# Hybrid SSD / attention / HGRN2 trunk: masked B in the F tile, a reordered last FFN column, later adaLN ticks, zero states by DMA

## The chip, the cores and the metric

The kernel runs on one core of a Trainium2 chip. The metric is the device time of one execution in microseconds (us); the time before is the median of three runs.

## The reference

The trunk has two layers over 256 context tokens and 1024 latent tokens of width 1024, all in float32. Each layer is a mixer and an FFN, both between RMS norms and with adaLN (shift, scale and gate from a conditioning vector). The mixer projects the tokens, and feeds three groups of heads: a Mamba-2 state space model (SSD) in both directions, a neighbourhood attention, and HGRN2. Their outputs are concatenated and projected.

```python
u = modulate(rmsnorm(h, norm_mix_pre), m[0], m[1])
a = mixer_block(u, ...)                  # u @ w_in -> [SSD | NA | HGRN2] -> concat @ w_out
h = h + m[2] * rmsnorm(a, norm_mix_post)
v = modulate(rmsnorm(h, norm_ffn_pre), m[3], m[4])
gate, up = split(v @ w_up)               # 1024 -> 2 x 2816
f = (silu(dwconv(gate)) * up) @ w_down   # 2816 -> 1024
h = h + m[5] * rmsnorm(f, norm_ffn_post)

def step(h, inp):                        # SSD, chunks of 128 tokens, 8 heads in 2 groups, states 64 x 64
    x_c, b_c, c_c, a_c = inp
    cum = cumsum(a_c)
    decay = exp(where(causal, cum[:, None] - cum[None], -inf))
    scores = einsum('btgn,bsgn->btsg', c_c, b_c)
    y = einsum('btsg,btsgh,bsghp->btghp', scores, decay, x_c)
    y = y + einsum('btgn,bghnp->btghp', c_c, h) * exp(cum)
    h = exp(cum[-1]) * h + einsum('bsgn,bsgh,bsghp->bghnp', b_c, exp(cum[-1:] - cum), x_c)
    return h, y
```

The states `h` start at zero in the context, in both directions. The latent scan starts from the context's last state. Layer 1 needs no outputs for the context.

## The kernel before

TensorE works on float32 operands that are split in two rounded parts, H and L; a product is made of three (HH, HL, LH). The 1280 tokens are ten tiles of 128. In each layer the input projections are interleaved with the HGRN2 and attention bodies; then `ssd_x` forms the states of all chunks and stores them to the DRAM tensor `hsD` (`hsD<-D_Us` in the trace), and `ssd_body` forms the outputs, chunk by chunk. `ssd_body` is woven with `out_first`, the half of the output projection that needs only attention and HGRN2 results: its matmuls are `g_p<-F_wo,U_m` and `g_p<-w_wo,U_m`. `out_second` does the rest, and the FFN follows.

In `ssd_body` a chunk goes as follows. `ssd_load` (L1271) takes a D tile `sc` ([128, 5, 512]) and an F tile `xz`, loads the two directions' states into `u[:, 0]`, the inputs x dt into `u[:, 1]` and x and z into `xz`. For the first chunk of a direction it sets the states to zero by a memset (L1278). `pmask` (L1268, on GpSimd) then writes three masked copies: the rows of decays (`S_R`), the columns (`D_sv`), and B of the two groups into `u[:, 4]`. `ssd_weights` (L1293), once per group, makes five matmuls for the exponents (`S_R`, `scr`), ScalarE's exponents, GpSimd's sum of two of them (`S_E<-S_E,S_E`, L1313), the exponent `ei` in `u[:, 2 + g]`, and the product of B and C from the masked B (`m_p<-F_cv,D_sc`, 128x128). `ssd_outputs` makes 16 matmuls per group out of the states and inputs (`m_p<-S_E,D_sc` and `m_p<-D_sc`). `ssd_gate` multiplies by z in the F tile (GpSimd, `F_xz<-F_xz`, L1333) and `ssd_squares` (L1342) sums squares with VectorE and a small matmul (`m_p<-cf,F_xz`).

The FFN goes up column tile by column tile of 128. Tiles 2 to 21 are made by `ffn_seven`, seven block products P1 to P7 in the manner of Strassen and Winograd; the parameter `late` puts the plain blocks first. The results `hid` go to DRAM. The way down (`ffn`, from L1725) has five passes over the token tiles; `load_wd` loads a row tile of `w_down` in two halves (`wr_wrd`), ScalarE and VectorE split it into a U tile (`U_dw`), and `values` loads and splits `hid` (`S_hL<-hid`, `S_hH`). In layer 0, `ada_tick` calls in between work on the adaLN modulation of layer 1: a tile of `in_ada_w` (`wr_aw`) and 16 matmuls per pair (`m_p<-wr_aw,scol`).

A scheduler fixes the order of the instructions of each engine ahead of time, by its own estimate of when each can run; `high_priority` moves `ssd_outputs` and the adaLN matmuls forward. Tiles come from pools with fixed numbers of buffers: U 10, F 10, D 3, wr 4, w 4, S 8, E 3. A tile waits until the last user of its buffer is done. All DMAs are issued by SyncE (SP) on one queue, in program order of that engine.

Of the kernel before, what the change touches and what calls it, by code (L numbers as in the profile page):

```python
# [23 lines left out]
NFF = DFF // 128  # L24
# [43 lines left out]
def drain(gen):  # L68

    while True:  # L70
        try:
            next(gen)
        except StopIteration as e:
            return e.value
# [54 lines left out]
class Kern:  # L129
# [1140 lines left out]

    def ssd_load(self, c, rows, cols, B):  # L1271
        tsl = slice(128 * c, 128 * c + 128)
        u = self.t("D", [128, 5, 512], name="sc")
        xz = self.t("F", [128, 2, 4, 128], name="xz")
        for d, i in ((0, c), (1, ORD_B.index(c))):
            hp = slice(64 * d, 64 * d + 64)
            if i == 0:
                self.nc.gpsimd.memset(u[hp, 0, :], 0.0)  # L1278
            else:
                self.dma(u[hp, 0, :], self.hsD[i, hp, :])  # L1280
        self.dma(u[:, 1, :], self.xtD[tsl, :])
        self.dma(xz[:, 0], self.xD[:, :, tsl].rearrange("j p t -> p j t"))
        self.dma(xz[:, 1], self.zD[:, :, tsl].rearrange("j p t -> p j t"))
        r = self.t("S", [128, 4, 128], F32R, name="R")
        self.pmask(r, rows[:, tsl].bitcast(F32), self.scs[:, 0:4], 4)
        o = 512 * (c % 2)
        cs = cols[:, 1, o:o + 512].rearrange("p (a b) -> p a b", b=128)
        self.pmask(cs, cols[:, 0, tsl].bitcast(F32), self.scs[:, 4:8], 4)
        o = 128 * c + (1 if c < 2 else 2)
        self.pmask(u[:, 4, 0:256].rearrange("p (a b) -> p a b", b=128), B[:, o:o + 128], self.scs[:, 8:10], 2)  # L1290
        return u, xz, r, cs

    def ssd_weights(self, Cm, c, g, u, r, cs):  # L1293

        o0 = 128 * c + (1 if c < 2 else 2)
        csl = slice(o0, o0 + 128)
        Es = []
        for d in range(2):
            ps = self.p("m")
            self.mm(ps, cs[:, 2 * g + d, :], r, stop=False)  # L1300
            self.mm(ps, self.identr, self.late[d].unsqueeze(1).to_broadcast([128, 4, 128]), start=False)
            e = self.t("S", [128, 4, 128], name="E")
            self.act(e.rearrange("p a b -> p (a b)"), ps, AF.Exp)
            Es.append(e)
        ps = self.p("m")
        self.mm(ps, self.sel[g], r)
        ei = u[:, 2 + g, :]
        self.act(ei, ps, AF.Exp)
        ei = ei.rearrange("p (h t) -> p h t", h=4)
        pg = self.p("m")  # L1310
        self.mm(pg[:, 0:128], u[:, 4, 128 * g:128 * g + 128], Cm[g][:, csl])
        w = Es[0]
        self.nc.gpsimd.tensor_tensor(out=w, in0=w, in1=Es[1], op=ALU.add)  # L1313
        self.nc.vector.tensor_tensor(out=ei, in0=ei, in1=Cm[g][:, csl].unsqueeze(1).to_broadcast([128, 4, 128]), op=ALU.mult)
        self.tt(w, w, pg[:, 0:128].unsqueeze(1).to_broadcast([128, 4, 128]), ALU.mult)
        return w, ei
# [399 lines left out]
    def ffn(self, l, v, blocks, C):  # L1716


        plain = self.ffn_plain(l, v, blocks, C, 1)
        next(plain)  # L1720
        op, rest = self.ffn_sums(v, len(blocks) == 3)
        drain(plain)
        rest()
        for j in range(2, NFF):
            drain(self.ffn_seven(l, v, op, blocks, C, j, j == 2))  # L1725

        self.facc = acc = self.new_acc(blocks)
        tiles = range(BLK[blocks[0]][0] // 128, NT)
        last = len(PASSES) - 1
        jobs = {p: [(j, "U" if p < last else "Fw"[i % 2]) for i, j in enumerate(grp)] for p, grp in enumerate(PASSES)}  # L1730
        W = {p: [] for p in jobs}
        def more(p):
            if p in jobs and jobs[p]:
                W[p].append(self.load_wd(l, *jobs[p].pop(0)))
        while jobs[0]:
            more(0)
        for p, grp in enumerate(PASSES):
            if p == last:
                yield 0.0
            n = len(grp)  # L1740
            def values(tt):
                L = self.t("S", [128, 5, 128], F32R, name="hL")[:, 0:n, :]
                H = self.t("S", [128, 5, 128], F32R, name="hH")[:, 0:n, :]
                x = L.bitcast(F32)
                self.dma(x, self.hidD[p][tt])
                self.split(H, L, x, "a")
                return H, L
            nxt = values(tiles[0])
            for i, tt in enumerate(tiles):
                H, L = nxt  # L1750
                if i + 1 < len(tiles):
                    nxt = values(tiles[i + 1])
                for q in range(2):
                    pp = self.p("m")
                    c = slice(512 * q, 512 * q + 512)
                    k = 0
                    for jj, (wH, wL) in enumerate(W[p]):
                        for a, w in ((H, wH), (L, wH), (H, wL)):
                            self.mm(pp, a[:, jj, :], w[:, c], start=(k == 0), stop=(k == 3 * n - 1))
                            k += 1  # L1760
                    a = self.half(acc(tt), q)
                    if p == 0:
                        self.acopy(a, pp)
                    else:
                        self.tt(a, a, pp, ALU.add)
                    if p < last:
                        self.ada_tick()
                if p == 1:
                    self.ada_tick()
                if i % 2 == 0:  # L1770
                    more(p + 1)
                if p == last:
                    yield 1.4 * n
            while p + 1 in jobs and jobs[p + 1]:
                more(p + 1)


    def run(self):
        A = self.A
        self.adaD, self.adaP, self.adaN, self.ada_pend, self.ada_todo = {}, {}, {}, [], []  # L1780
        self.consts()
        self.cond()
        X = [self.first_norm(0)]
        Wi = self.load_wt(0, *HEAD[0])
        mod = self.first_mod()
        Wh = Wi, self.load_wt(0, *HEAD[1])
        X.append(self.first_norm(1))
        U = {0: self.xn_to_u(0, X[0], mod)}
        X.append(self.first_norm(2))
        for b in (1, 2):  # L1790
            U[b] = self.xn_to_u(b, X[b], mod)
        C = {0: self.layer_cols(0)}
        self.lower_bounds()
        h1 = [self.dram([T, DM], f"h1_{l}") for l in range(2)]
        h2 = self.dram([T, DM], "h2")
        self.mixD = self.dram([8, 128, T], "mixD")
        self.zD = self.dram([4, 128, T], "zD")
        self.xD = self.dram([4, 128, T], "xD")
        self.accD = self.dram([T, DM], "accD")
        self.uD = self.dram([KT, 128, T], "uD")  # L1800
        self.hidD = [self.dram([NT, 128, len(grp), 128], f"hid{p}") for p, grp in enumerate(PASSES)]
        self.gD = self.dram([2, 128, T], "gD")
        self.iD = self.dram([T, 256], "iD")
        self.xtD = self.dram([T, 512], "xtD")
        self.vD = self.dram([T, 256], "vD")
        self.cvD = self.dram([2, 32, T], "cvD")
        self.hsD = self.dram([NT, 128, 512], "hsD")
        self.ada_todo = [(0, i, kt, q) for i in (1, 2) for q in range(4) for kt in range(KT)]
        for l in range(2):
            clo = 0 if l == 0 else 2  # L1810
            lat = [0, 1, 2] if l == 0 else [1, 2]
            U = self.layer(l, U, C, clo, lat, h1, h2, Wh)
# [21 lines left out]
    def layer(self, l, U, C, clo, lat, h1, h2, Wh):  # L1834
# [34 lines left out]
        if l == 0:  # L1869
            C[1] = self.layer_cols(1)  # L1870
            self.ada_todo = [(1, i, kt, q) for i in range(3) for q in range(4) for kt in range(KT)]
        ffn = self.ffn(l, v, lat, C[l])
        next(ffn)
        acc2 = self.facc
        self.ada_flush()
        gates = self.gate_rows(l, 5, A["norm_ffn_post"][l], need_ctx, "U")
        if l == 0:
            mod = self.mod_cols(1, 0, C[1]["nmp"])
            U, first, second = self.post(acc2, lat, hm, lambda tt: h2[128 * tt:128 * tt + 128, :], gates, mod, 5)
            self.dtr = self.t("O", [128, NT, 16], name="dtr")  # L1880
            overlap(ffn, 2, first, second, self.head(1, U, self.dtr, None))
            return U
# [32 lines left out]
```

## Time and profile before

| | |
|---|---|
| median of three runs | 3196.54 us (3195.41 to 3197.57) |
| the profiled execution, its own time | 3187.19 us |
| its span in the trace | 3185.4 us |
| mean granted clock of TensorE, of full speed | 0.971 |
| instructions | 55707 |
| DMA | 373.60 MB |

The span is what the trace covers; the time of the execution lies 1.8 us above it. TensorE (PE) is the engine of matmuls, DVE is VectorE, ACT ScalarE, POOL GpSimd. PEld is the load of weights into TensorE, which overlaps the matmuls. A granted clock of 1.00 stands for 2.4 GHz, 0.50 for 1.2 GHz. A row names the line of the kernel, the engine, the operation, and the tiles written and read (`out<-in`). The line of a helper such as L189 (the matmul) serves the whole kernel, so the tiles tell which part it is.

### The profile page before, as it was taken

The page shows a single profiled execution, that of the slowest core. Times are in us where ns is not written, and L with a number is a line of the kernel's source. Part 1 is how long each engine was busy: PE and PEld are TensorE (multiplying, and loading weights), DVE is VectorE, ACT ScalarE, POOL GpSimd, SP SyncE. Part 2 cuts the span into 40 slices and gives each one's busy share as a digit, 9 for nine tenths or more (in the row PEclk, how much of TensorE's full clock was granted, in tenths as well). Part 3 has the DMA queues.
Part 4 walks back from the last instruction along what each step waited for, and adds up shares of the span by engine and source line. Part 5 has one row for each costly group of instructions (what it writes and reads, how often), then busy time and mean ns, then how long its engine had stood idle before and what let it go on. Part 6 is the DMA issues. An engine that isn't in the chain of part 4 may idle for free. (4 is left out here: it accounts for less than half of the span.)

```text
span 3185.4 us, 55707 instructions
## 1 busy us (share of the span) xinstructions
PE 3010.9 (95%) x21478; PEld 2478.2 (78%) x21478; DVE 1874.8 (59%) x3568; ACT 1347.4 (42%) x2603; POOL 782.0 (25%) x849
## 2 busy tenths in 40 slices
PE   6999999979899999998999899999989999999997
PEld 4977777767778888886777797777767788887886
DVE  5263644668876655562335826555658876667347
ACT  5235525644643333342112633646545634445212
POOL 2000101246423333320000500101254554442002
PEclk9999999989999999999999899999989999999999
DMA  6333232456552222235564312231457532224242
GB/s 237 87 103 96 66 102 87 133 172 197 195 172 65 78 66 72 65 101 171 158 201 144 119 44 79 59 82 50 139 166 226 166 96 80 80 81 150 81 133 93
DMA packets 440650, 373.60 MB, mean 117 GB/s; under 512 B 28188, under 2 KB 360880, under 8 KB 439360
## 3 DMA queue, kind: packets, MB, share of 16 engines
q1 hardware_dynamic: 440384, 370.04, 38.3%
q8 instruction: 169, 2.77, 0.4%
q14 instruction: 97, 0.79, 0.1%
HBM read 265.17 MB, written 95.30 MB: 113 GB/s over the span
## 5 line engine op out<-in xcount | busy, mean ns | idle before, releaser
L189 PE MATMUL m_p<-U_dw,S_hH 128*128 128x512 f32 x1296 | 407.3, 394 | 1.7 <-ACT S_hH L171 1.7
L189 PE MATMUL m_p<-U_uH,w_wo 128*128 128x512 f32 x1120 | 302.5, 392 | 1.7 <-ACT w_wo L171 1.2
L189 PE MATMUL g_p<-U_uH,w_wH 128*128 128x512 f32 (+1 forms) x1192 | 285.6, 372 | 18.7 <-POOL U_uH L481 11.2
L189 PEld LDWEIGHTS m_p<-U_dw,S_hH 128*128 128x128 f32 x1296 | 243.4, 188 | 58.1 <-issue 4.2
L189 PE MATMUL g_p<-U_uL,w_wH 128*128 128x512 f32 (+1 forms) x1192 | 271.7, 364 | 0.0
L189 PE MATMUL g_p<-U_uH,w_wL 128*128 128x512 f32 (+1 forms) x1192 | 264.0, 358 | 0.0
L189 PE MATMUL m_p<-U_dw,S_hL 128*128 128x512 f32 x648 | 255.8, 395 | 1.9 <-DVE S_hL L177 1.9
L189 PEld LDWEIGHTS g_p<-U_uH,w_wH 128*128 128x128 f32 x1192 | 206.6, 197 | 60.6 <-POOL U_uH L481 20.0
L189 PEld LDWEIGHTS m_p<-U_uH,w_wo 128*128 128x128 f32 x1120 | 207.6, 188 | 46.2 <-ACT w_wo L171 1.6
L189 PEld LDWEIGHTS g_p<-U_uL,w_wH 128*128 128x128 f32 x1192 | 204.0, 197 | 31.6 <-issue 3.2
L189 PEld LDWEIGHTS g_p<-U_uH,w_wL 128*128 128x128 f32 x1192 | 200.7, 192 | 30.9 <-issue 1.4
L177 DVE TENSOR_TENSOR w_wo<-wr_wr,w_wo 128x512 fp32r<-128x512 f32 x168 | 147.8, 881 | 102.7 <-ACT w_wo L171 102.0
L189 PE MATMUL m_p<-D_su,w_wo 128*128 128x512 f32 x800 | 206.6, 394 | 0.0
L186 DVE SCALAR_TENSOR_TENSOR F_fc<-F_raw,colB,F_fc 128x1281 f32<-128x1281 f32 (+3 forms) x102 | 168.1, 1648 | 45.5 <-ACT F_fc L168 45.3
L171 ACT CAST S_hH<-S_hL 128x512 fp32r<-128x512 f32 (+1 forms) x90 | 59.7, 663 | 290.4 <-DMA S_hL<-hid 244.3
L177 DVE TENSOR_TENSOR S_hL<-S_hL,S_hH 128x512 fp32r<-128x512 f32 (+1 forms) x90 | 69.5, 772 | 191.3 <-ACT S_hH L171 191.1
L189 PEld LDWEIGHTS m_p<-D_su,w_wo 128*128 128x128 f32 x800 | 148.5, 187 | 33.9
L171 ACT CAST w_wo<-wr_wr 128x512 fp32r<-128x512 f32 x168 | 103.6, 620 | 158.2 <-PE m_p L189 101.8
L189 PE MATMUL m_p<-F_su,w_wo 128*128 128x512 f32 x640 | 161.4, 394 | 0.0
L1623 POOL TENSOR_TENSOR wr_t<-E_wr,E_wr 128x512 f32<-128x512 f32 x40 | 57.7, 1443 | 388.1 <-DMA E_wr<-in_ffn_w_up 347.9
L189 PE MATMUL m_p<-U_uL,w_wo 128*128 128x512 f32 x560 | 150.5, 390 | 0.0
L189 PEld LDWEIGHTS m_p<-U_dw,S_hL 128*128 128x128 f32 x648 | 121.9, 188 | 31.6 <-DVE S_hL L177 2.6
(372 smaller groups left out, 6267.0 us busy)
## 6 DMA issues: line engine op xcount, KB each, us to landing
wr_aw<-in_ada_w SPq DMA_DIRECT2D x160, 256.0 KB
wr_wr<-in_ffn_w_up SPq DMA_DIRECT2D x96, 256.0 KB
wr_wr<-in_w_in SPq DMA_DIRECT2D x88, 256.0 KB
wr_wrd<-in_ffn_w_down SPq DMA_DIRECT2D x88, 256.0 KB
E_wr<-in_ffn_w_up SPq DMA_DIRECT2D x80, 256.0 KB
hid<-S_u SPq DMA_DIRECT2D x80, 256.0 KB
S_hL<-hid SPq DMA_DIRECT2D x54, 256.0 KB
h<-D_acc SPq DMA_DIRECT2D x45, 256.0 KB
```

Of the source, the lines that this page charges most:

```text
L171: self.nc.scalar.copy(out, in_)
L177: self.nc.vector.tensor_tensor(out=out, in0=a, in1=b, op=op)
L186: self.nc.vector.scalar_tensor_tensor(out=out, in0=a, scalar=s, in1=b, op0=op0, op1=op1)
L189: self.nc.tensor.matmul(out, lhsT=lhsT, rhs=rhs, start=start, stop=stop)
L1623: padd = lambda o, x, y, op=ALU.add: gp.tensor_tensor(out=o, in0=x, in1=y, op=op)
```

## The change

There are four edits. First, `ffn_seven` takes the order `late` for the last column tile too (j = 21), so the products go P1, P2, P4, P6, P7, P5, P3 in place of P1, P6, P2, P7, P5, P4, P3. Second, the adaLN ticks in the way down start at the third token tile of the first pass, and pass 2 gets a third tick per tile as pass 1 has. Third, the masked B of a chunk is written behind x and z in the F tile (1280 columns in place of 1024), and the D tile shrinks from five to four rows of 512. Fourth, the zero states are read from `hsD[0]`, which one memset and one store fill at the start of the program; the two memsets of 64x512 go.

```diff
--- before.py
+++ after.py
@@ -1270,14 +1270,12 @@
 
     def ssd_load(self, c, rows, cols, B):
         tsl = slice(128 * c, 128 * c + 128)
-        u = self.t("D", [128, 5, 512], name="sc")
-        xz = self.t("F", [128, 2, 4, 128], name="xz")
+        u = self.t("D", [128, 4, 512], name="sc")
+        f = self.t("F", [128, 1280], name="xz")
+        xz, mb = f[:, 0:1024].rearrange("p (s j t) -> p s j t", s=2, j=4), f[:, 1024:1280]
         for d, i in ((0, c), (1, ORD_B.index(c))):
             hp = slice(64 * d, 64 * d + 64)
-            if i == 0:
-                self.nc.gpsimd.memset(u[hp, 0, :], 0.0)
-            else:
-                self.dma(u[hp, 0, :], self.hsD[i, hp, :])
+            self.dma(u[hp, 0, :], self.hsD[i, hp, :])
         self.dma(u[:, 1, :], self.xtD[tsl, :])
         self.dma(xz[:, 0], self.xD[:, :, tsl].rearrange("j p t -> p j t"))
         self.dma(xz[:, 1], self.zD[:, :, tsl].rearrange("j p t -> p j t"))
@@ -1287,10 +1285,10 @@
         cs = cols[:, 1, o:o + 512].rearrange("p (a b) -> p a b", b=128)
         self.pmask(cs, cols[:, 0, tsl].bitcast(F32), self.scs[:, 4:8], 4)
         o = 128 * c + (1 if c < 2 else 2)
-        self.pmask(u[:, 4, 0:256].rearrange("p (a b) -> p a b", b=128), B[:, o:o + 128], self.scs[:, 8:10], 2)
-        return u, xz, r, cs
-
-    def ssd_weights(self, Cm, c, g, u, r, cs):
+        self.pmask(mb.rearrange("p (a b) -> p a b", b=128), B[:, o:o + 128], self.scs[:, 8:10], 2)
+        return u, xz, r, cs, mb
+
+    def ssd_weights(self, Cm, c, g, u, r, cs, mb):
 
         o0 = 128 * c + (1 if c < 2 else 2)
         csl = slice(o0, o0 + 128)
@@ -1308,7 +1306,7 @@
         self.act(ei, ps, AF.Exp)
         ei = ei.rearrange("p (h t) -> p h t", h=4)
         pg = self.p("m")
-        self.mm(pg[:, 0:128], u[:, 4, 128 * g:128 * g + 128], Cm[g][:, csl])
+        self.mm(pg[:, 0:128], mb[:, 128 * g:128 * g + 128], Cm[g][:, csl])
         w = Es[0]
         self.nc.gpsimd.tensor_tensor(out=w, in0=w, in1=Es[1], op=ALU.add)
         self.nc.vector.tensor_tensor(out=ei, in0=ei, in1=Cm[g][:, csl].unsqueeze(1).to_broadcast([128, 4, 128]), op=ALU.mult)
@@ -1722,7 +1720,7 @@
         drain(plain)
         rest()
         for j in range(2, NFF):
-            drain(self.ffn_seven(l, v, op, blocks, C, j, j == 2))
+            drain(self.ffn_seven(l, v, op, blocks, C, j, j in (2, NFF - 1)))
 
         self.facc = acc = self.new_acc(blocks)
         tiles = range(BLK[blocks[0]][0] // 128, NT)
@@ -1763,9 +1761,9 @@
                         self.acopy(a, pp)
                     else:
                         self.tt(a, a, pp, ALU.add)
-                    if p < last:
+                    if p < last and (p, i) >= (0, 2):
                         self.ada_tick()
-                if p == 1:
+                if p in (1, 2):
                     self.ada_tick()
                 if i % 2 == 0:
                     more(p + 1)
@@ -1805,6 +1803,9 @@
         self.vD = self.dram([T, 256], "vD")
         self.cvD = self.dram([2, 32, T], "cvD")
         self.hsD = self.dram([NT, 128, 512], "hsD")
+        zero = self.t("S", [128, 512], name="zero")
+        self.nc.gpsimd.memset(zero, 0.0)
+        self.dma(self.hsD[0], zero)
         self.ada_todo = [(0, i, kt, q) for i in (1, 2) for q in range(4) for kt in range(KT)]
         for l in range(2):
             clo = 0 if l == 0 else 2
```

The pools and the scheduler decide what this does to the order. On TensorE, in the SSD loop of layer 0, at the fifth chunk, before (`m_p<-S_R` and `scr` are exponents, `m_p<-F_cv` with `D_sc` the product B·C, `g_p` the output projection):

```order
L189 MATMUL m_p_7997<-S_R_7993,D_sv_6601 128x512
L189 MATMUL m_p_7997<-scr_70 128x512
L189 MATMUL m_p_8002<-S_R_7993,D_sv_6601 128x512
L189 MATMUL m_p_8002<-scr_70 128x512
L189 MATMUL m_p_8007<-S_R_7993,scr_70 128x512
L189 MATMUL m_p_8010<-F_cv_6478,D_sc_7986 128x128
L189 MATMUL m_p_8031<-S_R_7993,D_sv_6601 128x512
L189 MATMUL m_p_8031<-scr_70 128x512
L189 MATMUL g_p_7942<-F_wo_7932,U_m_7378 128x512
L189 MATMUL g_p_8050<-F_wo_7932,U_m_7378 128x512
```

and now the five exponents and the start of the projection:

```order
L189 MATMUL m_p_8000<-S_R_7996,D_sv_6604 128x512
L189 MATMUL m_p_8000<-scr_70 128x512
L189 MATMUL m_p_8005<-S_R_7996,D_sv_6604 128x512
L189 MATMUL m_p_8005<-scr_70 128x512
L189 MATMUL m_p_8010<-S_R_7996,scr_70 128x512
L189 MATMUL g_p_8053<-F_wo_7925,U_m_7381 128x512
L189 MATMUL g_p_7945<-F_wo_7935,U_m_7381 128x512
L189 MATMUL g_p_8053<-F_wo_7935,U_m_7381 128x512
L189 MATMUL g_p_7945<-F_wo_7935,U_m_7381 128x512
L189 MATMUL g_p_8053<-F_wo_7935,U_m_7381 128x512
```

The projection goes on there without a break, 113 matmuls in all, and the chunk's product (now from `F_xz`) comes behind the last of them:

```order
L189 MATMUL g_p_8748<-w_wo_8706,U_m_7613 128x512 x2
L189 MATMUL g_p_8748<-w_wo_8716,U_m_7613 128x512 x2
L189 MATMUL g_p_8748<-w_wo_8707,U_m_7613 128x512 x2
L189 MATMUL g_p_8748<-w_wo_8717,U_m_7613 128x512 x2
L189 MATMUL m_p_8013<-F_cv_6481,F_xz_7990 128x128
L189 MATMUL m_p_8034<-S_R_7996,D_sv_6604 128x512
L189 MATMUL m_p_8034<-scr_70 128x512
L189 MATMUL m_p_8039<-S_R_7996,D_sv_6604 128x512
L189 MATMUL m_p_8039<-scr_70 128x512
L189 MATMUL m_p_8044<-S_R_7996,scr_70 128x512
```

So the product stands behind the block, and the exponents of the second group and all later chunks with it; the fourth chunk's last outputs too. In layer 1 the same happens with 88 matmuls.

On GpSimd, at the same chunk, before (`S_R` and `D_sv` are the masks of decays, `S_E` the sum of exponents, `F_cv,scs 128x256` the mask of B):

```order
L1268 TENSOR_TENSOR D_sv_6601<-D_sv_6601,scs_73 128x512
L1268 TENSOR_TENSOR S_R_7993<-F_sr_6599,scs_73 128x512
L1313 TENSOR_TENSOR S_E_7906<-S_E_7906,S_E_7911 128x512
L1268 TENSOR_TENSOR D_sc_7986<-F_cv_6042,scs_73 128x256
L1313 TENSOR_TENSOR S_E_8000<-S_E_8000,S_E_8005 128x512
L1333 TENSOR_TENSOR F_xz_7735<-F_xz_7735 128x512
L1268 TENSOR_TENSOR D_sv_6601<-D_sv_6601,scs_73 128x512
L1268 TENSOR_TENSOR S_R_8085<-F_sr_6599,scs_73 128x512
L1313 TENSOR_TENSOR S_E_8034<-S_E_8034,S_E_8039 128x512
L1268 TENSOR_TENSOR D_sc_8078<-F_cv_6042,scs_73 128x256
```

and now:

```order
L1268 TENSOR_TENSOR S_R_7996<-F_sr_6602,scs_73 128x512
L1311 TENSOR_TENSOR S_E_7909<-S_E_7909,S_E_7914 128x512
L1311 TENSOR_TENSOR S_E_8003<-S_E_8003,S_E_8008 128x512
L1331 TENSOR_TENSOR F_xz_7738<-F_xz_7738 128x512
L1268 TENSOR_TENSOR F_xz_7990<-F_cv_6045,scs_73 128x256
L1268 TENSOR_TENSOR F_xz_8082<-F_cv_6045,scs_73 128x256
L1268 TENSOR_TENSOR F_xz_8190<-F_cv_6045,scs_73 128x256
L1268 TENSOR_TENSOR F_xz_8282<-F_cv_6045,scs_73 128x256
L1268 TENSOR_TENSOR D_sv_6604<-D_sv_6604,scs_73 128x512
L1268 TENSOR_TENSOR S_R_8088<-F_sr_6602,scs_73 128x512
L1311 TENSOR_TENSOR S_E_8037<-S_E_8037,S_E_8042 128x512
L1268 TENSOR_TENSOR F_xz_8406<-F_cv_6045,scs_73 128x256
```

The masks of four chunks stand together now, and ahead of the next chunk's decays (`D_sv`, `S_R`).

On SP, at the end of FFN up in layer 1, before, the loads of `w_down` and the first load of `hid`:

```order
L164 DMA wr_wrd_28774<-in_ffn_w_down 128x512
L164 DMA wr_wrd_28778<-in_ffn_w_down 128x512
L164 DMA wr_wrd_28827<-in_ffn_w_down 128x512
L164 DMA wr_wrd_28831<-in_ffn_w_down 128x512
L164 DMA wr_wrd_28914<-in_ffn_w_down 128x512
L164 DMA S_hL_28782<-hid_158_617 128x640
L164 DMA wr_wrd_28918<-in_ffn_w_down 128x512
```

and now:

```order
L164 DMA wr_wrd_28830<-in_ffn_w_down 128x512
L164 DMA wr_wrd_28834<-in_ffn_w_down 128x512
L164 DMA wr_wrd_28917<-in_ffn_w_down 128x512
L164 DMA wr_wrd_28921<-in_ffn_w_down 128x512
L164 DMA wr_wrd_29004<-in_ffn_w_down 128x512
L164 DMA wr_wrd_29008<-in_ffn_w_down 128x512
L164 DMA wr_wrd_29091<-in_ffn_w_down 128x512
L164 DMA S_hL_28785<-hid_158_617 128x640
L164 DMA wr_wrd_29095<-in_ffn_w_down 128x512
```

From the first `w_down` load of this FFN on, 13 stood ahead of that load of `hid`, and now there are 17.

## Rows read from the trace of the kernel before

**Rows 1.** The page of the profile, part 1, whole span.

```profile
PE 3010.9 (95%) x21478; PEld 2478.2 (78%) x21478; DVE 1874.8 (59%) x3568; ACT 1347.4 (42%) x2603; POOL 782.0 (25%) x849
```

**Rows 2.** The profile by engine and wait, PE, whole span: waited us, times, longest us.

```profile
PE m_p L189 <- POOL D_sc L1268: 13.6, 3, 7.1
...
PE m_p L189 <- DVE F_xz L1342: 3.3, 4, 1.4
```

**Rows 3.** The timeline, layer 0, first chunk: start us, us, engine, line, operation.

```profile
684.66 1.27 SPq L164 DMA_DIRECT2D hsD<-D_Us  x2
...
693.04 1.14 SPq L164 DMA_DIRECT2D D_sc<-hsD  x2
693.20 0.60 ACT L168 ACTIVATE D_sc<-m_p 128x512 f32<-128x512 f32 x1 [4.33 <-DMA hsD<-D_Us]
...
693.82 0.61 POOL L1268 TENSOR_TENSOR D_sc<-F_cv,scs 128x256 f32<-128x256 f32 x1
...
694.48 0.80 PE L189 MATMUL m_p<-F_cv,D_sc 128*128 128x128 f32 x2 [5.21 <-POOL D_sc L1268]
...
697.77 0.70 PE L189 MATMUL m_p<-S_E,D_sc 128*64 128x128 f32 x4
```

**Rows 4.** The timeline, layer 1, first chunk.

```profile
2349.08 3.13 SPq L164 DMA_DIRECT2D D_sc<-hsD  x4
...
2351.25 0.79 PE L189 MATMUL m_p<-F_cv,D_sc 128*128 128x128 f32 x2 [7.14 <-POOL D_sc L1268]
...
2354.53 0.70 PE L189 MATMUL m_p<-S_E,D_sc 128*64 128x128 f32 x4
...
2366.40 0.80 PE L189 MATMUL m_p<-F_cv,D_sc 128*128 128x128 f32 x2 [1.29 <-POOL D_sc L1268]
```

**Rows 5.** PE by line and form, 713 to 790 us: busy us, mean ns.

```profile
L189 PE MATMUL g_p<-F_wo,U_m 128*128 128x512 f32 x140 | 36.7, 398 | 0.0
```

**Rows 6.** Busy us of PE, PEld, DVE, ACT, POOL by window, layer 0, one chunk.

```profile
700.70:705.90 5.20, 5.02 (x48) 4.20 (x46) 4.94 (x9) 4.17 (x9) 4.45 (x4) 1.00 0.63 199
```

**Rows 7.** POOL by line and form, layer 0, 690 to 790 us.

```profile
L1313 POOL TENSOR_TENSOR S_E<-S_E,S_E 128x512 f32<-128x512 f32 x18 | 26.7, 1485 | 11.4 <-ACT S_E L168 11.4
L1333 POOL TENSOR_TENSOR F_xz<-F_xz 128x512 f32<-128x512 f32 x9 | 13.0, 1444 | 7.8 <-DVE F_xz L186 7.2 <-DVE srs L183 0.6
L1268 POOL TENSOR_TENSOR S_R<-F_sr,scs 128x512 fp32r<-128x512 f32 x8 | 8.8, 1095 | 0.0
L1268 POOL TENSOR_TENSOR D_sv<-D_sv,scs 128x512 fp32r<-128x512 f32 x7 | 8.5, 1216 | 3.0 <-PE m_p L189 2.9
L1268 POOL TENSOR_TENSOR D_sc<-F_cv,scs 128x256 f32<-128x256 f32 x9 | 5.5, 614 | 3.8 <-PE m_p L189 3.8
```

**Rows 8.** POOL's timeline, layer 1, two chunks.

```profile
2353.40 1.13 POOL L1268 TENSOR_TENSOR D_sv<-D_sv,scs 128x512 fp32r<-128x512 f32 x1 [0.97 <-PE m_p L189]
...
2361.14 1.49 POOL L1268 TENSOR_TENSOR D_sv<-D_sv,scs 128x512 fp32r<-128x512 f32 x1
...
2369.69 1.48 POOL L1268 TENSOR_TENSOR D_sv<-D_sv,scs 128x512 fp32r<-128x512 f32 x1
```

**Rows 9.** The same by window, layer 1, with PEclk after the engines.

```profile
2354.00:2364.00 10.00, 8.60 (x84) 7.07 (x83) 8.49 (x13) 5.36 (x11) 10.00 (x9) 0.93 0.48 141
2364.00:2374.00 10.00, 8.71 (x51) 6.90 (x50) 8.16 (x15) 5.30 (x10) 9.89 (x8) 0.66 0.47 146
```

**Rows 10.** PE waits, layer 0, end of FFN up, 1430 to 1450 us.

```profile
PE m_p L189 <- DMA wr_aw<-in_ada_w: 7.6, 3, 4.9
```

**Rows 11.** SP's timeline, layer 1, end of FFN up.

```profile
2914.82 5.64 SPq L164 DMA_DIRECT2D wr_wrd<-in_ffn_w_down  x5
2920.51 0.43 SPq L164 DMA_DIRECT2D S_hL<-hid  x1
```

**Rows 12.** PE's timeline there.

```profile
2924.42 0.73 PE L189 MATMUL m_p<-U_dw,S_hH 128*128 128x512 f32 x2 [1.17 <-ACT S_hH L171]
2927.01 0.50 PE L189 MATMUL m_p<-U_dw,S_hL 128*128 128x512 f32 x1 [1.85 <-DVE S_hL L177]
```

## The prediction

> **What bounds the kernel now.** I began with the busy times of the whole span: TensorE is busy for 95% of it, VectorE 59%, ScalarE 42%, GpSimd 25% [rows 1]. So what the change is worth lies in the five per cent in which TensorE stands still, and in stretches where it runs at the lower of its two clocks. The second view is TensorE's waits by engine: the mask of B (`pmask`, L1268) holds it for 13.6 us in 3 waits, the longest 7.1 [rows 2]. The third view, the timeline, says why: these waits are not for GpSimd's work. In layer 0 the stores of the states (`hsD<-D_Us`) are issued at 684.66, nothing touches the D tiles until about 693, and then within a microsecond the load of the states, ScalarE's exponent and the mask all start; the product B·C follows at 694.48 after 5.21 us of idleness [rows 3]. All three write into the D tile `sc`, whose buffer was held by the stored states. Layer 1 has the same picture with 7.14 us [rows 4]. The mask takes 0.61 us; it merely sits in the wrong tile. One more wait of 1.29 us for a mask stands at 2366.40.
>
> The fourth view is needed for what comes after: how the SSD loop keeps TensorE busy. Between 713 and 790 us, TensorE interleaves the chunks with 140 matmuls of the first half of the output projection, `g_p<-F_wo` [rows 5], which do not depend on the chunks. These I call filler. A chunk alone is little work: the window 700.70 to 705.90 holds the 48 matmuls of one chunk with no filler, 5.02 us busy of 5.20 at the full clock [rows 6]. GpSimd needs more for it: two sums of exponents, one gate, two masks of decays and the mask of B, by their means 2 x 1.485 + 1.444 + 1.095 + 1.216 + 0.614 = 7.34 us [rows 7]. In layer 1 one filler-poor stretch shows what that does: GpSimd is busy 10.00 and 9.89 us of two windows of 10, TensorE only 8.60 and 8.71, at granted clocks of 0.93 and 0.66 of 2.4 GHz [rows 9], and its masks of decays, one per chunk, start 7.74 and 8.55 us apart [rows 8]. A chunk without filler is thus bound by GpSimd; with filler it is not.
>
> **The change, part by part.** The count of TensorE's instructions stays the same, and so does GpSimd's but for the memsets. What matters is order.
>
> *Masked B in the F tile.* On the gain side the first products no longer wait for the D buffer. The outputs of the first chunk still do: their operands (the states and ScalarE's exponents) go to the D tile, free at 693.04 [rows 3]. With the exponent (0.60 us) and a product on VectorE behind it they may start near 695.5 in place of 697.77. I take 3 us for layer 0, 0.7 of it for work done at a higher clock; bounds 1 (only the order inside the wait changes) and 5 (all of the 5.21). In layer 1 the four loads occupy SP until 2352.2 [rows 4]; outputs start perhaps 1.8 us earlier than 2354.53, the 1.29 us wait goes, and part of the lower clock of the second window [rows 9] comes back, where (1 - 0.66) of the 8.71 busy us, 3.0, is the most. I take 1.8 + 1.3 + 2.4 = 5.5, bounds 3 and 7. Together **-8.5** (-4 to -12).
>
> On the loss side stands the order. The F pool has ten buffers. The F tile of layer 0's fifth chunk takes a buffer that the weights `F_wo` hold until their last matmul. Before, only the gate, late in the chunk, needed that tile; now the mask does, so the product B·C does, and the schedule puts all remaining filler, 113 matmuls, as one block ahead of that product; in layer 1 it is 88. At 36.7/140 = 0.26 us each [rows 5] these blocks last 30 and 23 us, in which the SSD work rests: in GpSimd's order the blocked mask stands in front of the next chunk's decays, so it cannot work ahead. Behind the block the chunks have next to no filler: half a chunk and four more in layer 0 (4.5), about 4 in layer 1, until the last chunk gets the second part of the projection again.
>
> Each such chunk costs 7.34 - 5.20 = 2.14 us by the layer 0 means [rows 6, 7]; by the periods of layer 1, (7.74 + 8.55)/2 - 5.20 = 2.95 [rows 6, 8]; at the other end nothing, if GpSimd got ahead of TensorE. I take 2.14, since it comes from the mean of many instructions, and keep 0 and 2.95. Layer 0: 4.5 x 2.14 = 9.6, plus the three further masks that now queue behind the first and delay the decays, 3 x 0.61 = 1.8, less a wait like the 1.4 us for the squares [rows 2] that the block covers: 10.0. Layer 1: 4 x 2.14 = 8.6, plus 3 masks, 1.8: 10.4. Together **+20.4** (2 to 29).
>
> GpSimd's price depends on its company. The sums of exponents, 1.49 us on average in layer 0 [rows 7], fall in windows where VectorE is busy 8.49 and 8.16 of 10 us when the chunk periods lengthen to about 8 [rows 8, 9]. The Trainium skill (Perfetto Trace Analysis, Optimizing Scalar/DVE Operations) says that GpSimd and VectorE share a read port of SBUF, so that moving work between them may gain nothing. By that rule the tail, in which both work on the same chunks with no pause, would go by the longer periods; the rows of layer 1 agree with it, and the third rival gives that time.
>
> *Last FFN column in the order P1, P2, P4, P6, P7, P5, P3.* The same seven products and the same operands, so no TensorE work is added; what moves is when U buffers come free, and with them the loads of `w_down` ahead of the first `S_hL`. In layer 0 the first down-projection matmul still has the same three pairs of adaLN tiles in front of it, whose loads make 7.6 us of waits [rows 10], and `S_hL` still stands behind them on SP: 0, bounds -2 and +2. In layer 1 SP now issues 17 `w_down` loads ahead of the first `S_hL` in place of 13. Five of them took 5.64 us [rows 11], so 4 more are 4.5 us if the queue is as full. Each also has a cast on ScalarE and a difference on VectorE, and the splitting of `S_hL` queues behind these. TensorE lost 1.17 + 1.85 = 3.0 us here [rows 12]. Part of the 4.5 is gained by the earlier start of those loads; I take **+3**, bounds -3 (the whole wait goes) and +8 (all 4.5, the splits, and a stretch at the lower clock).
>
> *adaLN ticks from the third token tile on.* These move 16 matmuls per tick of 2 columns, each short, and their loads, later within the same five passes. Their total is unchanged; the pass has `w_down` matmuls enough to cover them. Cost 0, and its one exposed place is the three waits above, inside those bounds.
>
> *Zero states from DRAM.* One memset of 128x512 and one store at the start, where TensorE waits for inputs anyway; two 64x512 memsets in layer 0 become loads. GpSimd stood idle ahead of its memset, so the memset itself cost nothing that can come back; two more loads of the kind that SP issued in 1.14 us for two [rows 3] sit on the path to the first outputs. That is inside the layer 0 bounds above.
>
> Sum: -8.5 + 20.4 + 0 + 3 = **+14.9 us**. The profiled execution took 3187.2 us and its span is 3185.4, so it would become 3202. The median of the runs, 3196.5, lies 9.3 above it; the change is carried to that: 3196.5 + 14.9 = **3211**.
>
> **The rivals.** A measurement of this kernel tells 0.2%, 6.4 us, from no change.
>
> A, faster: GpSimd keeps up behind the block. Then the tail costs the queued masks alone, 3.6 - 1.4 = 2.2 us, FFN nothing, and the early gains stand: -8.5 + 2.2 = -6.3, 3190; with the early gains at their end, 3187. It decides at a GpSimd time per chunk of 5.2 us or less. For it: in the one filler-free chunk GpSimd is busy 4.45 of 5.20 us and no more [rows 6]. Against it: a whole chunk's operations add up to 7.34 us by their means [rows 7], and the block keeps it from working ahead. Chance 0.15.
>
> B, no measurable change: early gains near 12 and a tail near 15, because the last chunks meet filler sooner than I count: about 3199. Also the case that the mask's move changes little on the chip because the F buffers come free earlier than the schedule thinks. The order within each engine is fixed, so I hold that for small. Chance 0.22.
>
> C, slower by more: the tail goes by the long periods, 2.95 x 8.5 + 3.6 - 1.4 = 27.3, the filler blocks wait for their own weights and for the 3-buffer drain of the projection's results, and FFN costs its 8: -8.5 + 27.3 + 8 = +27, 3223; with the early gains at 4, 3228. For it: the two clock readings below 1 in the only comparable stretch [rows 9]. Chance 0.23.
>
> The forecast itself, 3203 to 3218, has 0.40. Slower by over 0.2% is the forecast and C: 0.63. The range leaves out the better half of A and the far end of C: 3188 to 3228.
>
> **What would show it.** Right: no wait for L1268 ahead of the first chunk; a stretch of 23 to 30 us in both layers in which TensorE does only `g_p` at full clock and GpSimd nearly nothing; behind it windows in which GpSimd is near 10 of 10 and TensorE near 7, with waits of TensorE for `S_E` or `F_xz`, summing to some 20 us. In layer 1 the first `S_hL` load is issued after 17 `w_down` loads and TensorE's gap there grows from 3 to about 6 us. Wrong: chunks behind the block at 5 to 6 us each with TensorE busy throughout, or first outputs that start no earlier than 697.8 and 2354.5 counted on the clock of before.

## The result, and the profile after

The changed kernel is slower: 3237.83 us, median of 5 runs (3234.22 to 3249.28), against 3196.54 us for 5 runs of the kernel before. The ratio is 1.014, with a 95% interval of 1.0123 to 1.0157, which is 39 to 50 us. The direction was as forecast; the size was nearly three times the forecast 14.9 us, and lies outside the range. The profiled execution took 3234.22 us, its span is 3232.4 us.

The busy times of the whole span [rows 1] hardly moved; TensorE's share fell from 95 to 93%:

```profile
PE 3019.4 (93%) x21478; PEld 2480.3 (77%) x21478; DVE 1883.8 (58%) x3568; ACT 1348.4 (42%) x2605; POOL 777.0 (24%) x848
```

TensorE's waits [rows 2] no longer name the mask. In its place stand the sums of squares, the exponent, and the load of the states:

```profile
PE m_p L189 <- DVE F_xz L1340: 21.9, 9, 4.2
...
PE m_p L189 <- ACT D_sc L168: 7.8, 2, 4.9
...
PE m_p L189 <- DMA D_sc<-hsD: 3.4, 2, 2.1
```

Most of the time went in the two SSD loops. The busy times by window (columns as in [rows 6], PEclk after the engines) from the last states matmul to the last sum of squares, layer 0 and layer 1, first before:

```profile
675.60:797.70 122.10, 109.14 (x718) 89.63 (x712) 93.94 (x166) 60.29 (x114) 72.94 (x61) 0.96 0.58 176
2332.10:2429.60 97.50, 86.09 (x562) 69.90 (x558) 72.67 (x126) 48.93 (x92) 56.39 (x46) 0.93 0.61 183
```

and after:

```profile
680.90:820.30 139.40, 117.34 (x729) 94.18 (x726) 95.18 (x167) 60.29 (x114) 72.25 (x57) 0.93 0.52 158
2359.70:2473.00 113.30, 92.32 (x560) 74.18 (x555) 73.83 (x129) 49.48 (x94) 55.39 (x44) 0.88 0.54 160
```

Together 219.6 us became 252.7, **+33.1**. TensorE's idle time (length less busy) rose from 24.4 to 43.0 us, +18.7. Its busy time rose too, from 195.2 us to 209.7, +14.4, at mean granted clocks of 0.93 and 0.88 in place of 0.96 and 0.93. The clock is about 10 us of these 14.4: by the traces' record of the granted clock, TensorE was busy at the lower level (0.50) for 39.3 us of the two loops, and for 19.1 before. Work at that level takes nearly twice as long (one 128x512 matmul of the exponents follows the other after 0.43 us near 705 us, and after 0.23 us near 692 us at the full clock), so about half of the difference is the clock's. Some 3 us more are 12 matmuls of the projection that stood behind the last sum of squares of layer 0 and now stand ahead of it (240 `g_p` in that window, 228 before). The rest of the projection, behind the two loops, takes 71.1 us in place of 77.9. Counted to the end of the projection the loss of the two layers is 26 us.

A second loss lies behind the projection of layer 0. From its last matmul to the first block product of FFN up (the norms and the first two columns lie between) the changed kernel takes 92.6 us, where it was 83.4.

The forecast's picture is all there. In layer 0, the four masks that stand behind the block wait 19.34 us for it, and the masks of decays behind it start 7.21, 7.64 and 7.08 us apart (GpSimd's timeline):

```profile
750.28 2.33 POOL L1268 TENSOR_TENSOR F_xz<-F_cv,scs 128x256 f32<-128x256 f32 x4 [19.34 <-PE g_p L189]
755.31 1.04 POOL L1268 TENSOR_TENSOR D_sv<-D_sv,scs 128x512 fp32r<-128x512 f32 x1 [2.70 <-PE m_p L189]
...
762.52 1.49 POOL L1268 TENSOR_TENSOR D_sv<-D_sv,scs 128x512 fp32r<-128x512 f32 x1
...
770.16 1.49 POOL L1268 TENSOR_TENSOR D_sv<-D_sv,scs 128x512 fp32r<-128x512 f32 x1
...
777.24 1.03 POOL L1268 TENSOR_TENSOR D_sv<-D_sv,scs 128x512 fp32r<-128x512 f32 x1
```

The windows show the block, where GpSimd and VectorE do nothing, and the bare chunks behind it, where GpSimd is full, TensorE is not, and its clock falls; in the last of them (780 to 790) it is VectorE that is full, at 9.81, and GpSimd is at 5.69:

```profile
740.00:750.00 10.00, 10.00 (x44) 8.08 (x44) 0.00 (x0) 2.35 (x4) 0.00 (x0) 1.00 0.21 80
750.00:760.00 10.00, 10.00 (x72) 8.41 (x71) 3.78 (x8) 3.43 (x7) 7.02 (x9) 1.00 0.99 296
760.00:770.00 10.00, 8.10 (x86) 6.72 (x84) 9.03 (x13) 6.84 (x14) 10.00 (x8) 1.00 1.05 286
770.00:780.00 10.00, 7.26 (x54) 5.54 (x50) 8.45 (x14) 4.48 (x9) 10.00 (x9) 0.83 0.40 130
780.00:790.00 10.00, 5.83 (x50) 4.65 (x50) 9.81 (x20) 5.40 (x10) 5.69 (x5) 1.00 0.34 95
```

The gain at the first chunk is not there. TensorE makes both products at once, but the D tile comes free as late as before: the stores are issued at 689.99, the load and the exponent start at 698.4, 8.4 us later in both kernels, and the 5.21 us [rows 3] are now 2.89 + 1.35 us at the outputs (timeline, layer 0). In layer 1 the 7.14 us [rows 4] became 4.91 + 2.07.

```profile
689.99 1.28 SPq L164 DMA_DIRECT2D hsD<-D_Us  x2
...
698.47 0.60 ACT L168 ACTIVATE D_sc<-m_p 128x512 f32<-128x512 f32 x1 [4.26 <-DMA hsD<-D_Us]
...
699.12 0.57 PE L189 MATMUL m_p<-S_E,D_sc 128*64 128x128 f32 x4 [2.89 <-ACT D_sc L168]
...
701.04 0.69 PE L189 MATMUL m_p<-D_sc 128*64 128x128 f32 x4 [1.35 <-DMA D_sc<-hsD]
```

At the turn of the FFN in layer 1, seven loads of `w_down` in a row hold SP for 7.92 us ahead of the first `hid` load, where five took 5.64 [rows 11], and the gaps of 1.17 and 1.85 us [rows 12] are 4.43 and 3.06:

```profile
2954.35 7.92 SPq L164 DMA_DIRECT2D wr_wrd<-in_ffn_w_down  x7
2962.32 0.42 SPq L164 DMA_DIRECT2D S_hL<-hid  x1
```

```profile
2967.11 1.22 PE L189 MATMUL m_p<-U_dw,S_hH 128*128 128x512 f32 x2 [4.43 <-ACT S_hH L171]
2971.39 0.79 PE L189 MATMUL m_p<-U_dw,S_hL 128*128 128x512 f32 x1 [3.06 <-DVE S_hL L177]
```

### The profile page after: what moved, and what is told of

Same layout as the page of the kernel before. It is cut to its first block, busy times and chain, and to the rows that moved or that the text cites. A ratio compares the mean times of both kernels' runs of the same rounds, so it can differ in the third digit from the quotient of the medians.

```text
span 3232.4 us, 55660 instructions
## 1 busy us (share of the span) xinstructions
PE 3019.4 (93%) x21478; PEld 2480.3 (77%) x21478; DVE 1883.8 (58%) x3568; ACT 1348.4 (42%) x2605; POOL 777.0 (24%) x848
## 5 line engine op out<-in xcount | busy, mean ns | idle before, releaser
L189 PE MATMUL g_p<-U_uH,w_wH 128*128 128x512 f32 (+1 forms) x1192 | 288.3, 375 | 24.4 <-POOL U_uH L481 12.6
```

What stands on the lines that cost most here:

```text
L189: self.nc.tensor.matmul(out, lhsT=lhsT, rhs=rhs, start=start, stop=stop)
```

## The experiments

All ratios are to the kernel before on the same chip, with 95% intervals.

### One edit at a time

**The mask alone.** The kernel before with the third edit only (`mb` in the F tile).

> The kernel before with the one edit of the masked B in the F tile. Theory F (the F buffer that the output projection's weights hold puts all its matmuls in one block and leaves the later chunks bare): most of the loss is here, 30 to 36 us slower than before, with a block of about 26 us in each layer in which GpSimd and VectorE stand still, and chunks 7.5 to 8.5 us apart behind it. Theory O (the other edits shift the order of the whole program, and that costs): at most 15 us slower than before.

3229.44 us, ratio 1.011 (1.0097 to 1.0123), 31 to 39 us. The two SSD loops take 248.7 us, +29.1, with a block of 112 and one of 88 matmuls:

```profile
681.60:821.50 139.90, 117.63 (x729) 94.79 (x726) 94.14 (x167) 60.35 (x114) 73.36 (x58) 0.93 0.51 157
2360.20:2469.00 108.80, 89.84 (x562) 72.50 (x558) 70.62 (x128) 49.27 (x94) 55.26 (x44) 0.89 0.56 164
```

Theory F holds: this edit is most of the loss. The stretch behind the projection of layer 0 takes 88.8 us here, 5.4 more than before.

**Everything but the mask.** The changed kernel with `u[:, 4]` as before.

> The changed kernel with the masked B back in the D tile; the other three edits stay. Theory F: 5 to 12 us slower than before (3 us before 300 us of the span, the rest where FFN up turns to FFN down in layer 1), and no block in the SSD loops. Theory O: 25 to 40 us slower than before.

3205.06 us, ratio 1.0038 (1.0025 to 1.0051). The loops take 221.0 us, as before within what repeats, and the stretch behind the projection of layer 0 takes 83.5:

```profile
682.10:805.20 123.10, 109.59 (x717) 89.77 (x714) 96.10 (x166) 60.62 (x114) 71.97 (x60) 0.94 0.58 176
2341.90:2439.80 97.90, 85.01 (x562) 68.82 (x558) 73.00 (x126) 49.32 (x93) 56.39 (x46) 0.95 0.61 182
```

**The zero states alone.**

> The kernel before with the zero states from DRAM alone. In my forecast this edit cost nothing. Its instructions shift the scheduled order from the first twenty rows on, so if the 3 us that the changed kernel loses before 300 us of its span come from it, it is 2 to 6 us slower than before; if they come from elsewhere, within 2 us of it.

3192.76 us, ratio 0.9999 (0.9991 to 1.0008): nothing, as forecast. The 3 us that the profiled execution of the changed kernel loses early are no effect of this edit: at the first states matmul of layer 0 the kernel with the mask alone is later by as much, though its order up to there was not touched. Single executions differ by that.

**The last column alone** (`j in (2, NFF - 1)`), and **the ticks alone** (`(p, i) >= (0, 2)`, `p in (1, 2)`).

> The kernel before with the plain blocks first in the last FFN column, alone. If the loss of the other three edits (12 us) comes from this one: 5 to 10 us slower than before, and the two gaps at the first down-projection matmuls of layer 1 (1.17 and 1.85 us before, 4.43 and 3.06 us in the changed kernel) are of the longer kind. If it comes from the adaLN ticks: within 3 us of before, with the short gaps.

3196.35 us, ratio 1.0022 (1.001 to 1.0034), 3 to 11 us. In layer 1 the gaps at the first down-projection matmuls are 4.80 and 3.31 us, of the longer kind (TensorE's waits, 2900 to 2975 us):

```profile
PE m_p L189 <- ACT S_hH L171: 4.8, 1, 4.8
PE m_p L189 <- DVE S_hL L177: 3.3, 1, 3.3
```

In layer 0 the waits for `in_ada_w` fell from 8.0 to 5.4 us, but one of 2.9 us for `S_hH` took their place.

> The kernel before with the adaLN ticks from the third token tile on, alone. My forecast put it at nothing, within 2 us of it. The other three edits together cost 12 us, the late column alone 7.5, the zero states nothing; if the prices add up, this one costs 3 to 6 us, in the way down of layer 0.

3190.1 us, ratio 1.0003 (0.9989 to 1.0017). Nothing, so the expected 3 to 6 us fall. The four edits alone add up to 1.1 + 0.22 + 0.03 - 0.01 = 1.34%, inside the interval of the whole.

### Is it the F buffer?

**The mask in neither D nor F.** The exponents' tile of a group gets 128 more columns, and the mask of that group goes there:

```diff
-            e = self.t("S", [128, 4, 128], name="E")
+            e = self.t("S", [128, 5, 128], name="E")
+            if d == 0:
+                mb = e[:, 4, :]
+                self.pmask(e[:, 4:5, :], B[:, csl], self.scs[:, 8 + g:9 + g], 1)
+            e = e[:, 0:4, :]
```

> The changed kernel with the masked B in neither D nor F: each group's 128 columns go to the unused end of the tile that takes the group's exponents (two masks of 128x128 on GpSimd in place of one of 128x256). Theory F: no block, the filler lies between the chunks as before, 5 to 12 us slower than before because of the other edits, less what the earlier first product brings (0 to 5). A rival to F, that GpSimd's work in the SSD loop by itself sets the time wherever the masks are: as slow as the changed kernel, about 40 us.

3208.25 us, ratio 1.0051 (1.0039 to 1.0064), 12 to 20 us slower than before and some 30 faster than the changed kernel. The order has no block, and the stretch behind the projection of layer 0 takes 83.6 us. The loops (same windows) take 223.3 us:

```profile
687.20:809.20 122.00, 109.71 (x718) 89.50 (x714) 93.99 (x166) 59.99 (x114) 73.10 (x69) 0.96 0.58 177
2351.00:2452.30 101.30, 87.03 (x561) 70.68 (x558) 73.94 (x127) 49.60 (x94) 58.03 (x53) 0.92 0.58 176
```

This separates two terms of the sum. Against the run with the mask in D (221.0 us), taking it out of D brought nothing (+2.3). Against the changed kernel (252.7), the F buffer costs 29.4 us in these windows: 43.0 - 26.6 = 16.4 of idle time, and 209.7 - 196.8 = 12.9 of busy time. Of the latter the clock is (39.3 - 21.8)/2 = 8.8, since with the mask in S TensorE was busy at the lower level for 21.8 us; some 3 are the 12 matmuls that moved into the window. The rest of the projection is 5.1 us shorter in the changed kernel than here, so that up to its end the F buffer costs 24 us.

**No stores of the states.** Every chunk loads the zero states, so the D buffers need not wait (the recurrence between chunks is left out):

```diff
-            self.dma(u[hp, 0, :], self.hsD[i, hp, :])
+            self.dma(u[hp, 0, :], self.hsD[0, hp, :])
...
-                    self.dma(self.hsD[1:NT, hp, cs].rearrange("i p c -> p i c"),
-                             Us[hp, 0:NT - 1].rearrange("p i a b -> p i (a b)"))
+                    pass
```

> The zero-states kernel with the stores of the states left out and every chunk starting from zero states (its output lacks the recurrence between chunks; mask in the D tile as before). Theory D (the idle time ahead of the first chunk is the store that holds the D buffers, and the mask was only the first in the queue behind it): TensorE's gaps of 5.2 and 7.1 us ahead of the first chunk shrink to under 2 us each, and 8 to 13 us are won. Rival M (the mask itself is late): the gaps stay above 4 us.

3173.92 us, ratio 0.9958 (0.9943 to 0.9973), about 15 us won. TensorE's waits at the first chunk of layer 0, mask still in D:

```profile
PE m_p L189 <- POOL D_sc L1267: 1.3, 1, 1.3
```

In layer 1 the long gap is gone too (no wait there is over 0.9 us), and the loops take 205.4 us, 14.2 less than before. The granted clock rose with the gaps gone, to 0.98 and 0.96:

```profile
675.70:789.10 113.40, 107.15 (x718) 87.47 (x713) 95.18 (x166) 60.02 (x114) 74.86 (x60) 0.98 0.57 179
2320.00:2412.00 92.00, 85.15 (x562) 68.56 (x558) 73.75 (x126) 48.43 (x92) 57.78 (x46) 0.96 0.58 178
```

Theory D is shown: the stores hold the chunk's D tile, and the mask was one of three things that waited for it.

### What sets the pace of a bare chunk?

Without GpSimd's multiplication by z in `ssd_gate` (one line removed):

> The changed kernel without the multiplication by z in the SSD gate (one GpSimd instruction of 1.3 to 1.7 us per chunk; the output then lacks the gate). Theory G (behind the block a chunk is bound by GpSimd): the chunk periods behind the block fall from 7.6 to 8.1 us to 6.2 to 6.8, and the two loops are 8 to 14 us shorter together. Rival V (VectorE, or the chain from one engine to the next, sets the period): it stays above 7.2 us and less than 5 us are won.

> The kernel before without the same multiplication (the output lacks the gate). Where filler lies between the chunks GpSimd is not the bound, so by theory G this wins little: 0 to 5 us. Under rival V also little. If it wins as much as in the changed kernel, GpSimd bounds the SSD loops with filler too, and the block is not what made it so.

The changed kernel took 3224.36 us (ratio 1.0105, 1.0081 to 1.0129) and its loops 237.9 us, 14.8 less. The chunks behind the block of layer 0 are 5.95, 6.93 and 6.62 us apart, 0.8 less on average for an instruction of 1.3 us:

```profile
758.14 1.04 POOL L1268 TENSOR_TENSOR D_sv<-D_sv,scs 128x512 fp32r<-128x512 f32 x1 [2.70 <-PE m_p L189]
...
764.09 1.49 POOL L1268 TENSOR_TENSOR D_sv<-D_sv,scs 128x512 fp32r<-128x512 f32 x1
...
771.02 1.18 POOL L1268 TENSOR_TENSOR D_sv<-D_sv,scs 128x512 fp32r<-128x512 f32 x1 [0.49 <-PE m_p L189]
777.64 1.18 POOL L1268 TENSOR_TENSOR D_sv<-D_sv,scs 128x512 fp32r<-128x512 f32 x1 [0.61 <-PE m_p L189]
```

But the kernel before won as much: 3178.99 us (0.9968, 0.995 to 0.9985), its loops 205.5 us, 14.1 less, where 0 to 5 was expected. So this pair does not show that GpSimd matters only behind a block. The gate is also a link in the chain from a chunk's outputs to its sum of squares, for which TensorE waits in both kernels.

**The mask by ScalarE**, in the exponents' tile, on the kernel with the late column and the early `hid` load of the next part:

```diff
-                self.pmask(e[:, 4:5, :], B[:, csl], self.scs[:, 8 + g:9 + g], 1)
+                self.act(mb, B[:, csl], AF.Copy, scale=self.scs[:, 8 + g:9 + g])
```

> The late column with the early hid load, and the masked B made by ScalarE (two copies of 128x128 with a scale per partition) in the unused end of the exponents' tile, so that neither D nor F holds it and GpSimd has 0.6 us less work per chunk. Theory G (GpSimd's chain sets the pace of the chunks): 3 to 8 us faster than the same kernel with the mask in D, 12 to 17 us faster than before. If GpSimd's work matters only behind a block: within 3 us of the kernel with the mask in D.

3178.47 us, ratio 0.997 (0.9953 to 0.9987); the same kernel with the mask in D has 0.9972. Nothing won, so with filler between the chunks 0.6 us of GpSimd's work per chunk has no price. Whether a bare chunk's period is GpSimd's total or the chain through the gate stays open: the full windows of GpSimd speak for the first, the pair without the gate allows both. Neither is the whole of it. Counted by the sums of squares, the bare chunks behind the block take 7.0, 7.6, 8.1 and 10.4 us in layer 0 and 7.0, 8.1 and 10.0 in layer 1. In the last of each layer VectorE is busy 10.2 of 10.4 us and all of the 10.0, GpSimd only 5.1 and 7.1: there VectorE has the squares' norm and the weights of the next part of the projection to do besides the chunk. No run takes work from VectorE, so what that would be worth is not shown.

### The turn of the FFN

The first `hid` tile is loaded and split ahead of the last column (the first 5 columns, which it holds, are long in DRAM):

```diff
         for j in range(2, NFF):
+            if j == NFF - 1:
+                ahead = first(BLK[blocks[0]][0] // 128)
             drain(self.ffn_seven(l, v, op, blocks, C, j, j in (2, NFF - 1)))
...
-            nxt = values(tiles[0])
+            nxt = ahead if p == 0 else values(tiles[0])
```

> The same order of the last column, but the first hid tile of the way down is loaded and split ahead of that column. Theory Q (the first hid load stands behind 17 loads of w_down on SP, and the splits behind theirs): the gaps at the first down-projection matmuls of layer 1 go, 3 to 8 us faster than the late column alone. Rival S (the split w_down tiles themselves are late, whatever the order): the gaps stay and are now ended by the U tiles, within 2 us of the late column alone.

3180.86 us, ratio 0.9972 (0.996 to 0.9985): 15 us faster than the late column alone, twice what was expected, since layer 0 gains as well. In layer 1 the first gap is gone and 2.0 us of the second is left. Theory Q holds. Then with the old order of the last column:

> The kernel before (last column in its old order) with the first hid tile of the way down loaded and split ahead of the last column. If the early hid load alone makes the gain of the run that joined it with the late column: 6 to 12 us faster than before. If the late column is needed for it, because only then are enough w_down tiles there: 0 to 4 us faster, with the waits for in_ada_w in layer 0 as long as before (7.6 us).

3177.62 us, ratio 0.9959 (0.9944 to 0.9975). The late column is not needed. At the turn of layer 0, where before 8.0 us went in waits for `in_ada_w`, down-projection matmuls now cover the adaLN loads, and in layer 1 there is no wait:

```profile
PE m_p L189 <- DMA wr_aw<-in_ada_w: 0.9, 1, 0.9
```

**With the states' store in long rows** (`hsD` as [2, 128, NT, 256]), on top of that:

> The kernel with the early hid load, and the states kept in DRAM with the chunks of a row side by side, so that their store goes out in rows of 9 KB in place of 1 KB (the mask stays in the D tile). Theory D: the idle time ahead of the first chunk of each layer (5.2 and 7.0 us) is as long as that store takes to land; it shrinks to 2 to 5 us in each layer, and the kernel is 3 to 8 us faster than with the early hid load alone, 14 to 19 us faster than before. Rival: it is set by the loads and stores queued around it (accD, w_out), and stays within 1 us.

3173.75 us, ratio 0.9944 (0.9926 to 0.9961), the fastest version here that computes all of it. The stores now hold the D tile 7.75 us, where it was 693.04 - 684.66 = 8.38 [rows 3]:

```profile
689.64 1.09 SPq L164 DMA_DIRECT2D hsD<-D_Us  x2
...
697.39 1.36 SPq L164 DMA_DIRECT2D D_sc<-hsD  x2
```

The gaps are 4.58 and 6.24 us, a little under 1 us shorter, which is the rival's figure. The gain over the early `hid` load alone is not told apart, as the two intervals overlap.

## Why the prediction was wrong

**The reading that held.** That the F tile makes a block of the filler, that GpSimd stands behind it and that the chunks after it are bare was read off the order, and is what the runs show. GpSimd's pace was right as well for the first bare chunks: 7.34 us was forecast from the means [rows 7], and its masks of decays behind the block of layer 0 are 7.31 apart on average, if by some luck, for a sum of exponents took 1.73 us there in place of 1.485, and the last of the three periods has no mask of B. The zero states and the ticks cost nothing, as said.

**The step that failed most: "Together -8.5".** Measured: nothing (221.0 us with the mask in D, 223.3 with it in S, no block in either). The mask was the wait that the profile named, but [rows 3] show three writers of the D tile starting within one microsecond. I saw that, and still counted 3 and 5.5 us, because I asked when the first outputs could start and not what the next chunk would then wait for. They did start earlier, 9.1 us after the stores are issued in layer 0, where it was 13.1, and 9.7 in layer 1, where it was 13.0. The first sum of squares behind them was no earlier: it came 24.8 us after the stores in layer 0, 24.9 before, and in layer 1 25.0 us after them, 21.8 before. With the mask in S it is 25.2 and 25.7, with the mask in D 25.2 and 21.9. So in layer 1 the mask's leaving the D tile even made it later: VectorE's reduction for the squares now stands behind both products of the next chunk (3.20 us together), where it stood between them before. In layer 0 I take it that the second group's operands and the next chunk, which come through the same D tiles, hold it; no run separates that.

**The term that was too small: the tail, "+20.4".** Against the mask in S it is 29.4 us by the loops' windows and 24 up to the end of the projection. Its idle time, 16.4 us, is a little under the estimate. What was left out is the clock: along with the idle time the granted clock fell (0.83 from 770 to 780 us), and that added 8.8 us in the loops. In the tail I had counted nothing for it, though the readings of 0.93 and 0.66 [rows 9] stood beside the very chunks from which I took the upper price. The price of 2.14 us a chunk was too low as well, for it took GpSimd for the only bound: by the sums of squares a bare chunk took 8.3 us on average, 3.1 above the 5.20 and more than the upper price of 2.95, and in the longest ones it is VectorE that is full. There were 7 such chunks and not 8.5, which hid part of this.

**The term that was missing: what follows the loops.** The forecast put nothing on the way from the projection to the block products of FFN up in layer 0. It took 9.2 us more in the changed kernel and 5.4 more with the mask alone, and 81.8 to 83.6 us, about as before, with the mask in D or S and the gate in place. So the mask's move costs there too, if less without the gate (82.0 us with the mask in F, 78.1 with it in D). TensorE is idle for 16.8 us of that stretch in the changed kernel and for 13.4 with the mask alone, 9.3 before; what the added idle time comes from stays open.

**The turn of the FFN, "+3".** The mechanism is the one named, and the size was at the upper bound: the gaps alone grew by 4.5 us, and the last column alone costs 3 to 11 us by the runs. Here too the granted clock was lower, 0.66 in 15 us around these gaps (2964 to 2979 us), where it was 1.00 before.

Of the three rivals C was nearest, and its two price terms, the long tail and the turn at its worst, are the ones that came. It kept the early gain, and so ended at 3223. Added up, the gain that did not come (8.5), the tail (4 too little), the stretch behind the projection (9) and the turn (4 to 5, with 7.5 us for the late column alone) make the 26 us by which the forecast of 14.9 fell short of the 41.3 between the medians. They are read from single executions, which differ by several us, so that the sum comes out this well is in part luck.

## What to carry to other kernels

When a wait names an operation that writes a tile, look at everything else that starts at the same moment: if it all goes to one buffer, then moving one writer renames the wait. Before moving a small operand into another tile, look up who holds that tile's buffers and until when: here 256 columns tied a chunk's first product to the end of another stage, and the schedule did the rest. And price idle time on TensorE with the stretch at the lower clock that comes with it; here that was 8.8 us on top of 16.4. And look at what the engines do behind the part that is changed: about a fifth of this loss lay there.

## What was not expected of the hardware

The cost of the clock was half as large as the idle time that it came with (some 10 us for +18.7 us of idleness in the two loops). And a store of 576 KB times two took nearly as long in rows of 9 KB (7.75 us) as in rows of 1 KB (8.38 us), though the DMA packets in that time fell from 1321 to 300, so the size of the rows was not what made it long.
